# Opening a two-branch RWKV-7 and short-convolution layer on one core: the first block's inputs and projections ahead of those of the later blocks

## The chip, the cores and the metric

The kernel runs on one core of a Trainium2 chip. A core has a matrix engine (TensorE, PE in the profile), a vector engine (VectorE, DVE), a scalar engine (ScalarE, ACT), a general engine (GpSimd, POOL) and an engine that here issues all transfers (SyncE, SP). Each of them works through its own instructions in order and waits on semaphores for the others. The metric is device time in microseconds (us), lower is better; the median of the runs counts.

## What is computed

One layer of a hybrid encoder over 1152 tokens of width 1024: 1024 tokens of one prompt and 8 samples of 16 tokens. The parts that matter here:

```
h = rmsnorm(x, g_norm)
proj = h @ w_in                      # 81 column tiles of 128
pa_mix = pa + mu_shift * (pa_prev - pa)
r, k, v, w_lr, a_lr, z_a = split(pa_mix)
d = w_decay0 + tanh(w_lr) @ w_decay2         # w_lr, a_lr: 64 columns each
w = exp(-DECAY_SCALE * sigmoid(d))
a = sigmoid(w_iclr0 + a_lr @ w_iclr2)
y, S = wkv7_scan(wkv0, r, w, kh, a, v, kt)   # delta rule, 16 heads of 64
u = gc * xb ;  out_b = (gb * conv3(u) * silu(z_b)) @ w_o_b
x = x + (sigmoid(g_a) * out_a + sigmoid(g_b) * out_b) @ w_out
x = x + sigmoid(rmsnorm(x, g_ple) @ w_ple_gate) * (p @ w_ple)
```

## The kernel before

The tokens are cut into three blocks, in this order: `BLOCKS = [(0, 512), (1024, 128), (512, 512)]`, that is the first half of the prompt, all samples, the second half of the prompt. The nine input tiles `xt` (128 tokens by 1024) are normed token by token, transposed on TensorE into PSUM tiles `px`, scaled by `g_norm` and written as a high and a low half-precision part into `hx`, which stays in SBUF (`prologue`, L259 to L286). A dense product of one 128-column tile of `w_in` with one block (`dense_parts`, L162) is 8 steps over the model width with 3 matmuls each (high by high, high by low, low by high), 24 in all, 128x512 or for the samples 128x128. Their PSUM tiles are named after what they hold: `dl` the 128 columns of `w_lr` and `a_lr`, `dk`, `dr`, `dv`, `dz` those of one pair of heads, `dC`, `dx`, `dzb`, `dB` those of the convolution branch.

Every load of a weight tile (`load_w`, L143) takes one of two staging buffers `wst`, is split by ScalarE (`whi`) and VectorE (`wlo`), and frees its staging buffer after the second. `lora_in` (L288) makes from `dl` the two small factors `lrd` and `lra`, from which every later step takes its decay and its learning rate (`lod`, `loa`).

The kernel's order is: four input tiles loaded, the `dl` weights, `prologue(0)`, the weights of the first pair of heads, `cload` (constants), `lora_in(0)`, `prologue(1)`, `prologue(2)`, `lora_in(1)`, `lora_in(2)`. In this part a list scheduler places the instructions of every engine. `prologue` works there in groups of two input tiles.

Then the main stage begins (`go`, L887). For the other engines the list scheduler still decides, but TensorE's order is written by a planner: seven streams (generators) give out small pieces of work, each with the time after which its next piece may come, and the planner puts them in line by a clock `pe[0]` that it counts itself from the matmuls' sizes. Streams in order of precedence: `chain` (the serial recurrence, 144 chunks, PSUM tiles `c` and `u`), `tail` (output norm, `y` and `py`), `values`, `inverse` (`itt`, `ig`, `i`, `ie`, `if`), `scores` (`psc`), `prep` (the projections of one step, `dk`, `dr`, `dv`, `dz`), `conv` (the convolution branch, eight times). A step is one pair of heads and one block, 24 in all; a pair has 8, 2 and 8 chunks. Pieces of dense products (`DENSE`, `MORE`) fill the time in which no other piece is due. Which stream fills is a matter of pace:

```
behind = S_conv.cost / CONV_US < (chunks[0] + LEAD) / 144
fills.sort(key=lambda x: (x is S_conv) != behind)
```

`tail` waits by the planner's clock 11 us between the sum over `y` and the transposes `py`; `prep` waits before `dv` until the tail of two steps earlier is done. After the main stage come the gates (`dgb`, `dga`), the output products (`ob`, `oa`, `oc`) and the last projection (`pg`, `ple`); these are placed by the list scheduler again, and the first `dgb` products stand between the last chunks of the chain.

Of the kernel before, what the change touches and what calls it, by code (L numbers as in the profile page):

```python
# [9 lines left out]
F32 = mybir.dt.float32  # L10
# [61 lines left out]
def _build(nc, tc, I, O, top):  # L72
# [181 lines left out]
    def xload(i):  # L254
        tag, bufs = (("ar", 3), ("kbt", 2))[i % 2]
        xts[i] = wk.tile([128, D], F32, tag=tag, name=f"xt{i}", bufs=bufs)
        SP.dma_start(xts[i], I["x"][i])

    def prologue(bi):  # L259
        o, n = blk = BLOCKS[bi]  # L260
        for t0 in range(0, n // 128, 2):
            tn = min(2, n // 128 - t0)
            ms = small.tile([128, 2], F32, tag="msx", name=f"msx{bi}_{t0}")
            xs = []
            for i in range(tn):
                ti = o // 128 + t0 + i
                if ti not in xts:
                    xload(ti)
                xs.append(xts[ti])
                jk = cvp.tile([128, D], F16, tag="tb", name=f"jk{ti}", bufs=1)  # L270
                A.activation(jk, xs[i], AF.Square, accum_out=ms[:, i:i + 1])
            V.tensor_scalar(out=ms[:, :tn], in0=ms[:, :tn], scalar1=1.0 / D, scalar2=EPS, op0=ALU.mult, op1=ALU.add)
            rs = rsqrt(ms[:, :tn], tn, f"x{tn}")
            for i in range(tn):
                V.tensor_scalar(out=xs[i], in0=xs[i], scalar1=rs[:, i:i + 1], scalar2=None, op0=ALU.mult)
            sl = slice(t0 * 128, (t0 + tn) * 128)
            for k0 in range(0, KT, 2):
                ps = psp.tile([128, 2, 256], F32, tag="p", name=f"px{bi}_{t0}_{k0}")
                for k in range(2):
                    for i in range(tn):  # L280
                        PE.transpose(ps[:, k, i * 128:(i + 1) * 128], xs[i][:, (k0 + k) * 128:(k0 + k + 1) * 128], ident)
                for k in range(2):
                    hi, lo = (hT(k0 + k, blk, w)[:, sl] for w in range(2))
                    A.activation(hi, ps[:, k, :tn * 128], AF.Copy, scale=P("gn", k0 + k))
                    V.scalar_tensor_tensor(out=lo, in0=ps[:, k, :tn * 128], scalar=P("gn", k0 + k), in1=hi,
                                           op0=ALU.mult, op1=ALU.subtract)  # L286

    def lora_in(bi):  # L288
        o, n = blk = BLOCKS[bi]
        ps = dense(wl, blk, f"l{bi}")  # L290
        lm = tt(st_, "ta", f"lm{bi}", TA)[:, :n]
        mixed(ps, T_L, blk, lm, P("mu", T_L), mum[:, T_L:T_L + 1], mus[:, T_L:T_L + 1], f"l{bi}")
        A.activation(lm[0:64], lm[0:64], AF.Tanh)
        A.activation(lrd[0:64, o:o + n], lm[0:64], AF.Copy)
        A.activation(lra[64:128, o:o + n], lm[64:128], AF.Copy)
        V.tensor_tensor(out=lrd[64:128, o:o + n], in0=lm[0:64], in1=lrd[0:64, o:o + n], op=ALU.subtract)
        V.tensor_tensor(out=lra[0:64, o:o + n], in0=lm[64:128], in1=lra[64:128, o:o + n], op=ALU.subtract)

    sbd = [wk.tile([128, 128], F32, tag=f"sbd{i}", name=f"sbd{i}", bufs=1) for i in range(3)]
# [46 lines left out]
    def prep(f):  # L346
# [8 lines left out]
        smp, nch, npr, nm = f.smp, f.nch, f.npr, f.nm  # L355
        th = []
        for q, hb in (("d", 0), ("a", 1)):
            yield 2.0 * hb
            ps = psa.tile([128, 512], F32, tag="a", name="lo" + q + nm)
            lr = (lrd, lra)[hb]  # L360
            mm(ps[:, :n], s.lwh[:, hb, :], lr[:, o:o + n], start=True, stop=False)
            mm(ps[:, :n], s.lwl[:, hb, :], lr[:, o:o + n], start=False, stop=True)
            t = tt(st_, "ta", "th" + q + nm, TA)[:, :n]
            A.activation(t, ps[:, :n], AF.Tanh, scale=0.5 * IWS, bias=half[:, hb, j:j + 1])
            th.append(t)
        thd, tha = th
        G.tensor_scalar(out=thd, in0=thd, scalar1=1.0, scalar2=None, op0=ALU.add)
        cum = tt(st_, "ta", "cum" + nm, TA)[:, :n]
        sl, ns = (16, 8) if smp else (64, nch)
        V.tensor_tensor_scan(out=cum, data0=(scan_s if smp else scan_p), data1=thd, initial=0.0,  # L370
                             op0=ALU.mult, op1=ALU.add)
        pb = tt(st_, "ta", "pb" + nm, TA)[:, :ns * (sl + 1)].rearrange("p (c t) -> p c t", t=sl + 1)
        G.memset(pb[:, :, 0:1], 1.0)
        seg = lambda x: x.rearrange("p (c t) -> p c t", t=sl)
        A.activation(pb[:, :, 1:], seg(cum), AF.Exp, scale=-0.5 * CDEC)
        pt = small.tile([128, 8], F32, tag="pt", name="pt" + nm, bufs=4)
        G.tensor_copy(pt.unsqueeze(2)[:, :ns, :], pb[:, :, sl:sl + 1])
        pi = tt(st_, "ta", "pi" + nm, TA)[:, :n]
        A.activation(pi, cum, AF.Exp, scale=0.5 * CDEC)

        m = {}
        ahead = g == 2 and j + 1 < 8
        for q, t in (("k", T_K), ("r", T_R), ("v", T_V), ("z", T_ZA)):
# [14 lines left out]
            mixed(ps, t + j, blk, x, *mu, q + nm)  # L398
            m[q] = x
            if q == "r":  # L400
                x = m["k"]
# [342 lines left out]
    def conv(j):  # L744
        nm = f"{j}"
        cs = cvp.tile([128, NTOK], F32, tag="cv", name="cs" + nm, bufs=2)
        w = conv_w(j, 0)
        for o, n in BLOCKS:
            ps = yield from dense_parts(w, (o, n), f"C{nm}_{o}")
            A.activation(cs[:, o:o + n], ps, AF.Copy, scale=IWS * IWS)  # L750
        s3 = lambda x: x.rearrange("p (s t) -> p s t", t=16)
        cv = cvp.tile([128, NTOK], F32, tag="cv", name="cv" + nm, bufs=2)
        w = conv_w(j, 1)
        for o, n in BLOCKS:
            ps = yield from dense_parts(w, (o, n), f"x{nm}_{o}")
            u = cvp.tile([128, 514], F32, tag="cu", name=f"u{nm}_{o}", bufs=1)
# [20 lines left out]
        w = conv_w(j, 2)  # L777
        for o, n in BLOCKS:
            ps = yield from dense_parts(w, (o, n), f"zb{nm}_{o}")
# [5 lines left out]
        for o, n in BLOCKS:  # L785
            ps = yield from dense_parts(w, (o, n), f"B{nm}_{o}")
            V.scalar_tensor_tensor(out=zs[:, o:o + n], in0=ps, scalar=0.5 * IWS * IWS, in1=zs[:, o:o + n],
                                   op0=ALU.mult, op1=ALU.mult)
# [5 lines left out]
    for j in range(8):  # L794
        for g in range(3):
            f = St()
            f.j, f.g, f.blk, f.i, f.y_done = j, g, BLOCKS[g], len(steps), False
            f.kb_done = f.m_done = f.x_done = False
# [12 lines left out]
    prologue(1)  # L811
    prologue(2)
    lora_in(1)
    lora_in(2)

    class Stream:
        def __init__(self, kind):  # L820
            self.kind, self.at, self.gen, self.next, self.ready, self.cost = kind, 0, None, None, 0.0, 0.0
            self.till, self.banks = None, 0
            self.total = 8 if kind is conv else len(steps)

# [23 lines left out]
        def fill(self):  # L848
            return self.next in (DENSE, MORE)

    S_chain, S_tail, S_val, S_inv, S_scores, S_prep, S_conv = every = [
        Stream(k) for k in (chain, tail, values, inverse, scores, prep, conv)]
    may = {S_chain: lambda i: S_inv.at > i and S_val.at > i and S_tail.at >= i - 1,
# [3 lines left out]
           S_scores: lambda i: S_prep.at > i and (i < 3 or steps[i - 3].y_done),  # L857
           S_prep: lambda i: S_chain.at >= i - 3,
           S_conv: lambda i: True}
    CONV_US, LEAD = 8 * 46.4, 4.0  # L860

    def go():
        while True:
            for x in every:
                if x.gen is None and x.at < x.total and may[x](x.at):
                    x.gen = x.kind(x.at if x is S_conv else steps[x.at])
                    x.step()
# [318 lines left out]
```

## Time and profile before

| | |
|---|---|
| median of 3 runs | 1945.68 us (1945.39 to 3071.51) |
| profiled execution, its own time | 1941.51 us |
| its span | 1939.7 us |
| TensorE busy | 1814.9 us (94%) |
| VectorE busy | 1255.6 us (65%) |
| ScalarE busy | 811.8 us (42%) |
| mean granted TensorE clock | 0.988 |

One execution is profiled. The page gives each engine's busy time and cuts the span into 40 slices; the views of the trace give single instructions with start and length, the idle time ahead of one and what ended it (in square brackets), and the busy time of each engine in chosen stretches. "Granted clock" is the share of TensorE's full clock, 1.00 or 0.50 at a moment and a mean in between over a stretch.

### The profile page before, as it was taken

The numbers are of one execution on the slowest core, as the hardware profiler recorded it, in microseconds if no ns is written. First come the engines' busy times: TensorE is split into PE (matmuls) and PEld (weight loads), VectorE is DVE, ScalarE is ACT, GpSimd is POOL, SyncE is SP. The second block draws the span as 40 slices with busy tenths as digits, with TensorE's granted clock in tenths as the row PEclk, the third lists the DMA queues.
The fourth block names the chain that finished last, engine by engine and source line by source line (L and its number), as shares of the span: only waits on it lengthen the run. The fifth ranks groups of instructions, "written<-read, shape, count | busy, mean of one in ns | idle before, by whom it ended". The sixth has DMA issues, their size and how long they took to land. (4 is left out here: it accounts for less than half of the span.)

```text
span 1939.7 us, 37843 instructions
## 1 busy us (share of the span) xinstructions
PE 1814.9 (94%) x15374; PEld 1248.6 (64%) x15374; DVE 1255.6 (65%) x3225; ACT 811.8 (42%) x1877; POOL 219.1 (11%) x333
## 2 busy tenths in 40 slices
PE   4999999999999999999999998799999999999997
PEld 2565665565566566566556566455698777899766
DVE  7466878787787787787877777774223311444665
ACT  6344545545446446446446445343202211332321
POOL 1010211111111111111111111110000111200000
PEclk9999999999999999999999999899999999999999
DMA  6002011101101101101101100013313311142012
GB/s 217 22 23 76 22 48 42 34 30 60 39 30 50 50 30 50 50 30 37 60 29 37 41 18 15 32 46 94 99 44 96 99 44 33 56 144 87 9 35 78
DMA packets 43758, 103.57 MB, mean 53 GB/s; under 512 B 6208, under 2 KB 21440, under 8 KB 43584
## 3 DMA queue, kind: packets, MB, share of 16 engines
q1 hardware_dynamic: 43584, 101.17, 16.3%
q8 instruction: 120, 1.97, 0.4%
q14 instruction: 54, 0.44, 0.1%
HBM read 84.40 MB, written 16.74 MB: 52 GB/s over the span
## 5 line engine op out<-in xcount | busy, mean ns | idle before, releaser
L92 PEld LDWEIGHTS <-whip 128*128 128x128 f16 x1536 | 132.3, 99 | 72.2 <-issue 3.5
L653 POOL TENSOR_SCALAR Spt<-sbd,pt 128x128 f32<-128x128 f32 x128 | 86.7, 677 | 664.8 <-DVE sbd L669 642.5
L92 PEld LDWEIGHTS <-wlop 128*128 128x128 f16 x768 | 75.4, 98 | 61.1 <-issue 1.1
L669 DVE SCALAR_TENSOR_TENSOR sbd<-u,pt,Spt 64x64 f32<-64x64 f32 x256 | 72.1, 282 | 65.3 <-PE u L92 61.6
L595 ACT ACTIVATE bdgt<-ig 64x512 f16<-64x512 f32 (+1 forms) x208 | 106.5, 512 | 2.5
L659 ACT ACTIVATE yst<-c 64x128 f32<-64x128 f32 x144 | 38.8, 270 | 151.0 <-DVE xs L658 149.7
L92 PE MATMUL dx<-hx,whiX 128*128 128x512 f16 (+1 forms) x384 | 88.4, 326 | 4.7 <-ACT sho L229 4.7
L92 PE MATMUL dgb<-hx,whigb 128*128 128x512 f16 (+1 forms) x384 | 90.5, 331 | 2.2 <-ACT whigb L148 1.6
L92 PE MATMUL dv<-hx,whip 128*128 128x512 f16 (+1 forms) x384 | 90.7, 331 | 0.0
L92 PE MATMUL dzb<-hx,whiZ 128*128 128x512 f16 (+1 forms) x384 | 88.6, 326 | 2.2 <-ACT sho L229 1.8
L92 PE MATMUL dz<-hx,whip 128*128 128x512 f16 (+1 forms) x384 | 89.5, 326 | 0.0
L92 PE MATMUL dC<-hx,whiC 128*128 128x512 f16 (+1 forms) x384 | 88.4, 327 | 1.1 <-ACT cs L750 0.6
L92 PE MATMUL dB<-hx,whiB 128*128 128x512 f16 (+1 forms) x384 | 89.1, 326 | 0.0
L92 PE MATMUL pg<-xn,pg 128*128 128x384 f16 (+1 forms) x576 | 88.9, 309 | 0.0
L92 PE MATMUL dr<-hx,whip 128*128 128x512 f16 (+1 forms) x384 | 88.9, 326 | 0.0
L92 PE MATMUL dk<-hx,whip 128*128 128x512 f16 (+1 forms) x384 | 88.1, 326 | 0.0
L92 PE MATMUL dga<-hx,whiga 128*128 128x512 f16 (+1 forms) x384 | 86.9, 326 | 0.0
L92 PEld LDWEIGHTS <-pg 128*128 128x128 f16 x768 | 66.3, 99 | 27.1 <-issue 2.4
L664 ACT ACTIVATE vu<-u 64x64 f32<-64x64 f32 x288 | 62.3, 216 | 46.8 <-PE u L92 44.1
L589 ACT ACTIVATE gt<-ig 128x512 f16<-128x512 f32 (+1 forms) x104 | 54.3, 522 | 66.0 <-PE ig L92 65.1
L596 DVE CAST_PREDICATED tt<-cph,i 128x512 f16<-128x512 uint16 (+1 forms) x104 | 61.7, 593 | 25.4 <-PE i L92 24.3
L92 PEld LDWEIGHTS u<-xs,tm 128*128 128x128 f32 x288 | 49.7, 192 | 43.9 <-DVE xs L658 28.8
(325 smaller groups left out, 4924.8 us busy)
## 6 DMA issues: line engine op xcount, KB each, us to landing
wstp<-i_w_in SPq DMA_DIRECT2D x32, 512.0 KB, 3.6
xt<-i_x SPq DMA_DIRECT2D x9, 512.0 KB, 5.5
ob_d<-zb SPq DMA_DIRECT2D x8, 576.0 KB, 2.8
ostb<-ob_d SPq DMA_DIRECT2D x24, 192.0 KB, 3.1
osta<-oa_d SPq DMA_DIRECT2D x24, 192.0 KB, 2.9
xr<-i_xT SPq DMA_DIRECT2D x8, 576.0 KB, 3.6
wstC<-i_w_in SPq DMA_DIRECT2D x8, 512.0 KB, 3.5
wstX<-i_w_in SPq DMA_DIRECT2D x8, 512.0 KB, 3.5
```

The costliest lines, as they stand in the source:

```text
L92: PE.matmul(out, lhsT, rhs, start=start, stop=stop)
L589: A.activation(Gt, pg, AF.Copy, scale=-1.0)
L595: A.activation(Gb[R, :, R], pg[R], AF.Copy, scale=-1.0)
L596: V.copy_predicated(out=Tt, mask=bc(lvt[:, b, :]).bitcast(U16), data=p1)
L653: G.tensor_scalar(out=Spt, in0=S, scalar1=pt[:, c:c + 1], scalar2=None, op0=ALU.mult)
L659: A.activation(yst[Vh, p, :], pc[Vh, 0:128], AF.Copy)
L664: A.activation(vu[Uh, c, H], pu[H, H], AF.Copy, scale=-1.0)
L669: V.scalar_tensor_tensor(out=S2[H, H], in0=pu[H, 128 + h * 64:192 + h * 64], scalar=pt[H, c:c + 1], in1=Spt[H, H], op0=ALU.mult, op1=ALU.add)
```

## The change

The input tiles go to four buffer tags in place of two. `prologue` norms a whole block as one group (one sum, one reciprocal root for four tiles), scales every second tile on ScalarE, and is a generator that gives out one transposed column tile at a time. Block 0's prologue runs ahead under high priority; the `k` weights are loaded ahead of the `l` weights, then the constants, the small second factors, `C0`, `r`, the five other input tiles, `v` and `z`. An eighth stream `opening` does the rest: for block 0 it waits until `dk` of step 0 is out and does `lora_in(0)`; for the two other blocks it does their prologue and then `lora_in`. `prep` of step 0 takes `k` first and its decay part (`lod`, `loa`) after; `prep` of steps 1 and 2, the conv products of blocks 1 and 2 and `keys` wait until `opening` has come so far.

```diff
     def xload(i):
-        tag, bufs = (("ar", 3), ("kbt", 2))[i % 2]
+        tag, bufs = (("ar", 3), ("kbt", 2), ("vu", 2), ("scy", 3))[i % 4]
...
     def prologue(bi):
-        for t0 in range(0, n // 128, 2):
-            tn = min(2, n // 128 - t0)
...
+        tn = n // 128
+        ms = small.tile([128, 4], F32, tag="msx", name=f"msx{bi}")[:, :tn]
+        xs = [xts[o // 128 + i] for i in range(tn)]
...
+        rs = rsqrt(ms, tn, f"x{bi}")
+        for i in range(tn):
+            if i % 2:
+                A.activation(xs[i], xs[i], AF.Copy, scale=rs[:, i:i + 1])
+            else:
+                V.tensor_scalar(out=xs[i], in0=xs[i], scalar1=rs[:, i:i + 1], scalar2=None, op0=ALU.mult)
+        for k in range(KT):
+            yield 1.0 if k else (0.0, 9.0, 1.0)[bi], 1
+            ps = psp.tile([128, 512], F32, tag="p", name=f"px{bi}_{k}")[:, :n]
             for i in range(tn):
+                tr(ps[:, i * 128:(i + 1) * 128], xs[i][:, k * 128:(k + 1) * 128], ident)
+            hold(1.5)
+            A.activation(hT(k, blk, 0), ps, AF.Copy, scale=P("gn", k))
+            V.scalar_tensor_tensor(out=hT(k, blk, 1), in0=ps, scalar=P("gn", k), in1=hT(k, blk, 0),
+                                   op0=ALU.mult, op1=ALU.subtract)
...
     def lora_in(bi):
-        ps = dense(wl, blk, f"l{bi}")
+        yield 1.5
+        ps = yield from dense_parts(wl, blk, f"l{bi}")
...
+    def opening(i):
+        if i == 0:
+            yield lambda: steps[0].k_done
+        else:
+            yield waits[i]
+            yield from inputs[i]
+        yield from lora_in(i)
+        if i == 0:
+            inputs.extend([None, prologue(1), prologue(2)])
+            waits.extend([None, next(inputs[1]), next(inputs[2])])
...
+        def decay():
+            yield lambda: f.i or S_open.at > 0
...
+            if q == "k" and not f.i:
+                f.k_done = True
+                tha, pb, pt, pi = yield from decay()
...
-        yield lambda: f.i < 1 or steps[f.i - 1].kb_done
+        yield lambda: S_open.at == 3 and (f.i < 1 or steps[f.i - 1].kb_done)
...
         for o, n in BLOCKS:
+            yield lambda: o == 0 or S_open.at >= 2 + (o == 512)
             ps = yield from dense_parts(w, (o, n), f"C{nm}_{o}")
...
     for i in range(4):
         xload(i)
+    with tc.high_priority():
+        for _ in prologue(0):
+            pass
+    load_q(0, "k")
     wl = load_w(I["w_in"][T_L], "l")
-    prologue(0)
+    cload()
     load_lora(0)
-    for q in "krvz":
+    cws[0] = load_w(I["w_in"][T_C], "C0")
+    load_q(0, "r")
+    for i in (8, 4, 5, 6, 7):
+        xload(i)
+    for q in "vz":
         load_q(0, q)
-    cload()
-    lora_in(0)
-    prologue(1)
-    prologue(2)
-    lora_in(1)
-    lora_in(2)
...
-           S_prep: lambda i: S_chain.at >= i - 3,
+           S_prep: lambda i: S_chain.at >= i - 3 and S_open.at >= (0, 2, 3)[min(i, 2)],
+           S_open: lambda i: True,
```

The new stream stands in the planner's list between `scores` and `prep`.

What it moves on the engines is shown at three places. The first is VectorE at the very start, the reciprocal root (`nrx`, `nax`) and the scaling of the first input tiles. Before, for the group of two tiles:

```order
L138 SCALAR_TENSOR_TENSOR nax_159<-nax_159,nrx_158 128x2
L139 SCALAR_TENSOR_TENSOR nrx_158<-nax_159,nrx_158 128x2
L275 TENSOR_SCALAR xt_138<-xt_138,nrx_158 128x1024
L275 TENSOR_SCALAR xt_140<-xt_140,nrx_158 128x1024
L272 TENSOR_SCALAR msx_2_208<-msx_2_208 128x2
```

After, for the group of four:

```order
L137 TENSOR_TENSOR nax_157<-nrx_156,msx_146 128x4
L149 SCALAR_TENSOR_TENSOR wlop_8_231<-wstp_8_228,whip_8_230 128x1024
L138 SCALAR_TENSOR_TENSOR nax_157<-nax_157,nrx_156 128x4
L139 SCALAR_TENSOR_TENSOR nrx_156<-nax_157,nrx_156 128x4
L274 TENSOR_SCALAR xt_138<-xt_138,nrx_156 128x1024
L274 TENSOR_SCALAR xt_142<-xt_142,nrx_156 128x1024
L149 SCALAR_TENSOR_TENSOR wlol<-wstl,whil 128x1024
```

The split of the `k` weights now stands inside the reciprocal root, and only tiles 0 and 2 are scaled here; ScalarE scales 1 and 3 (after `whip_8` and `whil` in its own order).

The second place is TensorE where the first decay product `lod` of step 0 stands. Before, in the middle of the samples' `dl`:

```order
L92 LDWEIGHTS whil
L92 MATMUL dl_502<-hx,whil 128x128
L92 LDWEIGHTS lwh_269
L92 MATMUL lod_0_589<-lrd,lwh_269 128x512
L92 LDWEIGHTS lwl_270
L92 MATMUL lod_0_589<-lrd,lwl_270 128x512
L281 MATMUL px_0_6_375<-ident,xt_336 128x128 x2
L92 LDWEIGHTS whil
L92 MATMUL dl_502<-hx,whil 128x128
```

After, right behind the last matmul of block 0's `dl`, with `loa` and then `dr` behind it:

```order
L92 MATMUL dl_353<-hx,wlol 128x512
L92 LDWEIGHTS lwh_249
L92 MATMUL lod_0_430<-lrd,lwh_249 128x512
L92 LDWEIGHTS lwl_250
L92 MATMUL lod_0_430<-lrd,lwl_250 128x512
L92 LDWEIGHTS lwh_249
L92 MATMUL loa_0_435<-lra,lwh_249 128x512
L92 LDWEIGHTS lwl_250
L92 MATMUL loa_0_435<-lra,lwl_250 128x512
L92 LDWEIGHTS whip_0_261
L92 MATMUL dr_0_450<-hx,whip_0_261 128x512
```

So `lod` lost what stood between its input's product and itself. The third place is TensorE near the end of the main stage, where the output transposes `py` of the last pair's step before stand (`u` belongs to the chain, `ig` and `i` to the inverse). Before:

```order
L92 MATMUL u_0_1_16416<-vu_0_15726,kbt_0_15669 128x128
L92 LDWEIGHTS bdmh
L92 MATMUL ig_1_16435<-tt_1_16270,bdmh 128x64
L92 LDWEIGHTS bdmh
L92 MATMUL ig_1_16435<-tt_1_16270,bdmh 128x64
L96 MATMUL py_2_16440<-ident,yc_2_16327 128x128 x4
L92 LDWEIGHTS whip_16_14594
L92 MATMUL dv_2_16448<-hx,whip_16_14594 128x512
```

After:

```order
L92 LDWEIGHTS whiB_15629
L92 MATMUL dB_1024_16311<-hx,whiB_15629 128x128
L92 LDWEIGHTS whiB_15629
L92 MATMUL dB_1024_16311<-hx,whiB_15629 128x128
L92 LDWEIGHTS wloB_15630
L92 MATMUL dB_1024_16311<-hx,wloB_15630 128x128
L92 MATMUL u_0_1_16295<-vu_0_15492,kbt_0_15435 128x128
L96 MATMUL py_2_16321<-ident,yc_2_16155 128x128 x4
```

The last convolution product `dB` of the eighth convolution, which before was through some ten chunks earlier, now lies around this place: all 24 matmuls of its block 0, the first 6 of the samples' 24 ahead of `py`, the rest and block 2's 24 behind it.

## Rows read from the trace of the kernel before

**Rows 1.** Busy time by stretch: the stretch (us from the span's start), its length, then busy us and instructions of TensorE, its weight loads, VectorE, ScalarE and GpSimd, the granted TensorE clock, the transfer engines' share and GB/s.

```profile
0.00:26.00 26.00, 6.26 (x24) 4.57 (x25) 16.58 (x51) 14.96 (x25) 4.86 (x15) 1.00 0.79 270
26.00:60.00 34.00, 26.25 (x125) 15.64 (x125) 26.17 (x80) 22.43 (x54) 0.00 (x0) 0.85 0.30 103
60.00:160.00 100.00, 96.98 (x833) 54.78 (x832) 58.87 (x132) 42.29 (x88) 11.04 (x19) 1.00 0.11 35
160.00:1220.00 1060.00, 1003.66 (x9879) 635.52 (x9878) 836.15 (x2242) 534.24 (x1300) 158.88 (x258) 1.00 0.12 39
1220.00:1240.00 20.00, 11.78 (x100) 8.36 (x100) 15.75 (x60) 7.01 (x26) 1.71 (x2) 0.74 0.03 10
1240.00:1252.00 12.00, 11.26 (x69) 6.51 (x65) 6.71 (x18) 2.27 (x9) 1.21 (x2) 1.00 0.03 10
```

**Rows 2.** TensorE in order of time at the start: start us, length us, engine, line, operation, operands, count, and in brackets the idle time before and what ended it. The first transposes, the first dense product, the first matmul behind the last `dl`.

```profile
11.00 2.21 PE L281 MATMUL px<-ident,xt 128*128 128x128 f32 x8 [11.00 <-DVE xt L275]
...
26.05 0.59 PE L92 MATMUL dl<-hx,whil 128*128 128x512 f16 x1 [1.92 <-ACT hx L284]
...
59.97 0.38 PE L92 MATMUL dC<-hx,wloC 128*128 128x512 f16 x1
```

**Rows 3.** Groups of TensorE instructions from 0 to 60 us, shapes apart: busy us, mean ns of one, then idle us before them and what ended it. Of the three matmuls of each dense step two are `whil`, one `wlol`.

```profile
L281 PE MATMUL px<-ident,xt 128*128 128x128 f32 x72 | 16.8, 378 | 20.6 <-DVE xt L275 15.9 <-DVE hx L285 4.6
L92 PE MATMUL dl<-hx,whil 128*128 128x512 f16 x32 | 12.5, 448 | 3.2 <-ACT hx L284 2.5 <-DVE hx L285 0.7
...
L92 PE MATMUL dl<-hx,whil 128*128 128x128 f16 x16 | 3.3, 266 | 3.1 <-ACT hx L284 2.6 <-DVE hx L285 0.6
```

**Rows 4.** TensorE in order of time, to be read for the time from one start to the next: one 128x512 matmul in the first dense product, three of them a little later (two high, one low), three of 128x128, and four transposes.

```profile
27.72 0.63 PE L92 MATMUL dl<-hx,wlol 128*128 128x512 f16 x1
28.15 0.63 PE L92 MATMUL dl<-hx,whil 128*128 128x512 f16 x1
...
60.19 0.59 PE L92 MATMUL dC<-hx,whiC 128*128 128x512 f16 x2
...
60.83 0.59 PE L92 MATMUL dC<-hx,whiC 128*128 128x512 f16 x2
...
1197.48 0.28 PE L92 MATMUL dz<-hx,whip 128*128 128x128 f16 x2
...
1197.65 0.28 PE L92 MATMUL dz<-hx,whip 128*128 128x128 f16 x2
...
1245.70 0.64 PE L96 MATMUL prn<-ident,rnb 128*128 128x128 f32 x4
1246.18 0.59 PE L92 MATMUL dz<-hx,whip 128*128 128x512 f16 x2
```

**Rows 5.** The other engines at the start: ScalarE reading the sum of the fourth square, its first weight split, and a later split that waited for its load; VectorE's first step of the first reciprocal root (eleven steps), the two scalings behind it, and a weight split; SyncE's issue of the load that the later split waited for.

```profile
10.41 0.19 ACT L271 ACTIVATION_READ_ACCUMULATOR jk<-xt 128x1 f32 x1
11.04 1.06 ACT L148 ACTIVATE whil<-wstl 128x1024 f16<-128x1024 f32 x1 [0.44 <-DMA wstl<-i_w_in]
...
21.58 1.06 ACT L148 ACTIVATE whip<-wstp 128x1024 f16<-128x1024 f32 x1 [2.28 <-DMA wstp<-i_w_in]
...
8.02 0.17 DVE L272 TENSOR_SCALAR msx<-msx 128x2 f32<-128x2 f32 x1 [2.79 <-ACT jk L271]
...
10.19 1.42 DVE L275 TENSOR_SCALAR xt<-xt,nrx 128x1024 f32<-128x1024 f32 x2
...
12.20 1.23 DVE L149 SCALAR_TENSOR_TENSOR wlol<-wstl,whil 128x1024 f16<-128x1024 f32 x1
...
16.98 0.33 SPq L145 DMA_DIRECT2D wstp<-i_w_in  x1
```

**Rows 6.** From `dl` to `lod` of block 0, on ScalarE, VectorE and TensorE, each in order of time.

```profile
36.24 0.69 ACT L222 ACTIVATE lm<-dl,mum 128x512 f32<-128x512 f32 x1
...
38.17 0.62 ACT L293 ACTIVATE lm<-lm 64x512 f32<-64x512 f32 x1
...
39.47 0.63 ACT L294 ACTIVATE lrd<-lm 64x512 f16<-64x512 f32 x1
...
36.97 0.75 DVE L227 SCALAR_TENSOR_TENSOR lm<-dl,mus,lm 128x511 f32<-128x511 f32 x1
...
40.44 0.69 DVE L296 TENSOR_TENSOR lrd<-lm,lrd 64x512 f16<-64x512 f32 x1
...
41.18 0.38 PE L92 MATMUL lod<-lrd,lwh 128*128 128x512 f16 x1 [0.56 <-DVE lrd L296]
```

**Rows 7.** Busy time by stretch while transposes of block 2 stand between dense matmuls, and the stretch behind it (columns as in the first group).

```profile
48.00:56.00 8.00, 6.62 (x26) 4.11 (x26) 4.88 (x13) 4.46 (x12) 0.00 (x0) 0.57 0.00 0
56.00:60.00 4.00, 4.00 (x23) 2.03 (x22) 1.74 (x4) 1.36 (x4) 0.00 (x0) 1.00 0.00 0
```

**Rows 8.** TensorE and VectorE in order of time around `py` of the last pair: `c` products of the chain, and the transposes with their wait for the normed output `yc`.

```profile
1222.63 0.39 PE L92 MATMUL c<-sbd,ar 128*128 128x128 f32 x2
...
1236.08 1.11 PE L96 MATMUL py<-ident,yc 128*128 128x128 f32 x4 [4.84 <-DVE yc L723]
...
1239.55 0.47 PE L92 MATMUL c<-sbd,ar 128*128 128x128 f32 x2
...
1251.80 0.38 PE L92 MATMUL c<-sbd,ar 128*128 128x128 f32 x2
...
1235.35 0.68 DVE L723 TENSOR_TENSOR yc<-yc,nry 128x512 f32<-128x512 f32 x1
```

More of the change, by code (lines that the diff above doesn't have):

```diff
@@ L260, in prologue @@
         o, n = blk = BLOCKS[bi]
-        for t0 in range(0, n // 128, 2):
-            tn = min(2, n // 128 - t0)
-            ms = small.tile([128, 2], F32, tag="msx", name=f"msx{bi}_{t0}")
-            xs = []
-            for i in range(tn):
[L266 to L286, printed above, removed]
@@ new lines, in prologue @@
+        tn = n // 128
+        ms = small.tile([128, 4], F32, tag="msx", name=f"msx{bi}")[:, :tn]
+        xs = [xts[o // 128 + i] for i in range(tn)]
+        for i in range(tn):
+            jk = cvp.tile([128, D], F16, tag="tb", name=f"jk{bi}_{i}", bufs=1)
+            A.activation(jk, xs[i], AF.Square, accum_out=ms[:, i:i + 1])
+        V.tensor_scalar(out=ms, in0=ms, scalar1=1.0 / D, scalar2=EPS, op0=ALU.mult, op1=ALU.add)
+        rs = rsqrt(ms, tn, f"x{bi}")
+        for i in range(tn):
+            if i % 2:
+                A.activation(xs[i], xs[i], AF.Copy, scale=rs[:, i:i + 1])
+            else:
+                V.tensor_scalar(out=xs[i], in0=xs[i], scalar1=rs[:, i:i + 1], scalar2=None, op0=ALU.mult)
@@ L297, in lora_in @@
         V.tensor_tensor(out=lra[0:64, o:o + n], in0=lm[64:128], in1=lra[64:128, o:o + n], op=ALU.subtract)
+    def opening(i):
[8 more added lines that the diff above has]
+            waits.extend([None, next(inputs[1]), next(inputs[2])])
+    inputs, waits = [], []
     sbd = [wk.tile([128, 128], F32, tag=f"sbd{i}", name=f"sbd{i}", bufs=1) for i in range(3)]
@@ L355, in prep @@
         smp, nch, npr, nm = f.smp, f.nch, f.npr, f.nm
[L356 to L365, printed above, removed]
@@ L366, in prep @@
-        thd, tha = th
-        G.tensor_scalar(out=thd, in0=thd, scalar1=1.0, scalar2=None, op0=ALU.add)
-        cum = tt(st_, "ta", "cum" + nm, TA)[:, :n]
-        sl, ns = (16, 8) if smp else (64, nch)
[L370 to L379, printed above, removed]
+        sl, ns = (16, 8) if smp else (64, nch)
+        def decay():
+            th = []
+            yield lambda: f.i or S_open.at > 0
+            for q, hb in (("d", 0), ("a", 1)):
+                yield 2.0 * hb
+                ps = psa.tile([128, 512], F32, tag="a", name="lo" + q + nm)
+                lr = (lrd, lra)[hb]
+                mm(ps[:, :n], s.lwh[:, hb, :], lr[:, o:o + n], start=True, stop=False)
+                mm(ps[:, :n], s.lwl[:, hb, :], lr[:, o:o + n], start=False, stop=True)
+                t = tt(st_, "ta", "th" + q + nm, TA)[:, :n]
+                A.activation(t, ps[:, :n], AF.Tanh, scale=0.5 * IWS, bias=half[:, hb, j:j + 1])
+                th.append(t)
+            thd, tha = th
+            G.tensor_scalar(out=thd, in0=thd, scalar1=1.0, scalar2=None, op0=ALU.add)
+            cum = tt(st_, "ta", "cum" + nm, TA)[:, :n]
+            V.tensor_tensor_scan(out=cum, data0=(scan_s if smp else scan_p), data1=thd, initial=0.0,
+                                 op0=ALU.mult, op1=ALU.add)
+            pb = tt(st_, "ta", "pb" + nm, TA)[:, :ns * (sl + 1)].rearrange("p (c t) -> p c t", t=sl + 1)
+            G.memset(pb[:, :, 0:1], 1.0)
+            seg = lambda x: x.rearrange("p (c t) -> p c t", t=sl)
+            A.activation(pb[:, :, 1:], seg(cum), AF.Exp, scale=-0.5 * CDEC)
+            pt = small.tile([128, 8], F32, tag="pt", name="pt" + nm, bufs=4)
+            G.tensor_copy(pt.unsqueeze(2)[:, :ns, :], pb[:, :, sl:sl + 1])
+            pi = tt(st_, "ta", "pi" + nm, TA)[:, :n]
+            A.activation(pi, cum, AF.Exp, scale=0.5 * CDEC)
+            return tha, pb, pt, pi
@@ L381, in prep @@
+        if f.i:
+            tha, pb, pt, pi = yield from decay()
         m = {}
@@ L399, in prep @@
             m[q] = x
+            if q == "k" and not f.i:
+                f.k_done = True
+                tha, pb, pt, pi = yield from decay()
             if q == "r":
@@ L754, in conv @@
         for o, n in BLOCKS:
+            yield lambda: o == 0 or S_open.at >= 2 + (o == 512)
             ps = yield from dense_parts(w, (o, n), f"x{nm}_{o}")
@@ L822, in __init__ @@
             self.till, self.banks = None, 0
-            self.total = 8 if kind is conv else len(steps)
+            self.total = {conv: 8, opening: 3}.get(kind, len(steps))
         def step(self):
@@ L849, in fill @@
             return self.next in (DENSE, MORE)
-    S_chain, S_tail, S_val, S_inv, S_scores, S_prep, S_conv = every = [
-        Stream(k) for k in (chain, tail, values, inverse, scores, prep, conv)]
+    S_chain, S_tail, S_val, S_inv, S_scores, S_open, S_prep, S_conv = every = [
+        Stream(k) for k in (chain, tail, values, inverse, scores, opening, prep, conv)]
     may = {S_chain: lambda i: S_inv.at > i and S_val.at > i and S_tail.at >= i - 1,
@@ L865, in go @@
                 if x.gen is None and x.at < x.total and may[x](x.at):
-                    x.gen = x.kind(x.at if x is S_conv else steps[x.at])
+                    x.gen = x.kind(x.at if x in (S_conv, S_open) else steps[x.at])
                     x.step()
```

4 lines of the change are left out of this document (3 added, 1 removed).

## The prediction

> **What bounds the kernel now.** I read first the busy time by stretch. From 60 to 1220 us TensorE is the bound: it is busy 1003.66 of the 1060 us from 160 on, at the full clock, so 5.3% idle [rows 1], spread over small waits. The reader should see two places that stand out. In the first 60 us TensorE works for 32.5 us and much of that slowly; from 1220 to 1240 it is busy 11.78 of 20 us, at a mean clock of 0.74 [rows 1]. Then I read TensorE in order of time at both places, and the other engines beside it, to see who is late. What lies between is a long stretch in which the time is the matmul work plus a few per cent.
>
> So the sum is kept in one currency, the time lost: time passed, less the work that TensorE has done at its full clock. Work that only changes its place costs nothing; what is lost less is gained.
>
> Prices at the full clock come from the time between starts [rows 4]. Three 128x512 matmuls take 0.64 us (60.19 to 60.83), so 0.216 each; at the half clock one takes 0.43 (27.72 to 28.15). Three of 128x128 take 0.17 us, 0.057 each; four transposes 0.48, 0.12 each.
>
> **Lost at the start, before.** The first transposes start at 11.00, the first dense matmul at 26.05, and at 59.97 the last `dl` is through [rows 2]. By then TensorE has done all 72 transposes and the `dl` of the three blocks, 48 large and 24 small matmuls [rows 3], and by its order two `lod` and two `dC`: 72 x 0.12 + 52 x 0.216 + 24 x 0.057 = 21.2 us of work. Lost: 59.97 - 21.2 = 38.8 us. The transposes alone waited 20.6 us for scaled inputs and PSUM [rows 3].
>
> **Lost at the start, after.** The loads of the four tiles are the same, so the fourth square's sum is there at 10.6 [rows 5]. The first reciprocal root took from 8.02 to 10.19 for its eleven steps [rows 5]; now it starts at 10.7, and a weight split of 1.23 us stands in it, which waits for ScalarE's 1.06 us on the same weights (11.04 to 12.1, as `whil` before) and fits in at about 12.5. The root ends at 14.1; VectorE scales two tiles in 1.42, ScalarE (1.06 for a like tile [rows 5]) two from 14.1 to 16.2. First transposes at 14.8, so 3.8 later than before, and the first column tile is complete at about 16.6.
>
> From there eight column tiles go through two PSUM banks; each costs ScalarE about 0.69 and VectorE 0.75 (its nearest 128x512 rows [rows 6]). VectorE has between them two weight splits (1.23 each), one small one and the tail of the samples' sum: 6.0 + 2.5 + 0.6, from 17.3 to about 27. The `dC` weights: their load now waits for the `k` split to free a staging buffer (13.8); a load in this stretch took 16.98 to 21.58, 4.6 us [rows 5], so they are there at 18.4 and split by 22.3. `dC` can start at 21.5, waits a moment for the low weights, is paced by the last column tiles and starts at the half clock like the first `dl` (0.43): I take its end at 31. Work by then: 32 x 0.12 + 24 x 0.216 = 9.0; lost 22.0. That is 16.8 us less.
>
> Some of it is given back, because `opening` has little to fill with:
> - `lod` stands right behind `dl`. From ScalarE's start on `dl` to `lod` it took 36.24 to 41.18, 4.9 us, with a little foreign work in it [rows 6]. Before, TensorE filled this and waited 0.56; now nothing stands between. Queued behind `lod` are `loa`, `dr` and all else of TensorE, and the later engines wait with it. Price 4.7.
> - After a stop of 4.84 us at 1231 the matmuls from 1236.08 to 1239.55 ran at half speed [rows 8]. I expect the same in `dr`: half of 3.5, 1.8 us.
> - Behind `dr` stand three transposes, then the sums `pss`, which need ScalarE's mixed `r` (0.69, it stands ahead on ScalarE) and a square of like length, with two small evictions: about 2.2 against 0.4 us of transposes. Price 1.8.
> - The samples' `dl` waits for their last column tile behind `v`: 0.5. Block 2's transposes stand between `dz` matmuls; VectorE has there 8 evictions and some ten operations of `keys`, 13 us against TensorE's 9, but `dl` of block 2 fills behind: 1.5.
>
> Lost by the end of the third `dl`: 22.0 + 10.3 = 32.3 against 38.8, so the start gives **6.5 us**. Both ends: nothing, if the `dC` weights come some 6 us later, and 16.8 - 4.7 = 12 if the wait for `lod` is all that is given back.
>
> **The middle.** By the order, TensorE has between the first chunks of the third, fourth, fifth and sixth pair the same dense matmuls before and after (401, 392, 392, 392 large ones, 196 small). The chain only comes earlier: ahead of its first chunk stand 320 large dense matmuls in place of 386. Since TensorE and not the chain is the bound here, I cost this at nothing; what hides it is the dense work itself, and should the chain become the bound, rival 2's price is due. The fewer small operations (three reciprocal roots in place of five, 24 evictions an engine in place of 40) lie on engines that are 50 and 79% busy there [rows 1]: nothing.
>
> **The hole at 1220.** Before, the convolution branch is through by then, `dv` of the last step may not start before the tail two steps earlier is done, and TensorE stands for the chain and then 4.84 us for `yc`, which VectorE finishes at 1236.03 [rows 8]. From 1220 to 1252 TensorE is busy 23.0 of 32, so 9.0 idle [rows 1]. A mean clock of 0.74 over 20 us is 10.4 us at half, about 5 of them busy, so 2.5 us of work lost: 11.5 in all. Of this 1.7 (5.3% of 32) is usual and stays: at most 9.8 to gain. After, 48 large and 24 small `dB` matmuls, 11.7 us, are left for just this place, 24 and 6 of them ahead of `py`. They took their time earlier before, so what they fill here is saved there. The least: `py` still waits its 4.84 and 1.7 follow at the half clock, so 3.3. I take **8**, near the upper end, because VectorE's long list ahead of `yc` came from the next step's keys, whose `pss` now stands behind the chain's second chunk. The chain can follow: over the last pair's first six chunks TensorE now has 107 large dense matmuls by its order, 23 us, in place of 62, and a chunk there took 6.1 us with matmuls between (1239.55 to 1251.80 is two [rows 8]), 37 for six.
>
> What comes next is as before: `dz` of the last step ends at the chain's fifth chunk of that step in both orders, and the gates' weights follow it.
>
> **The sum.** 6.5 + 8 = 14.5 us. The profiled execution has a span of 1939.7 and a time of 1941.51: 1927.0. The median of the runs is 4.2 above that execution, so for the median **1931**.
>
> **Rivals.**
> 1. The start gives nothing: the change delays the first transposes, the `C0` load stands behind a staging buffer, and the first dense matmul comes so late that the waits eat it all. For it: constants and five input tiles are queued around it, and the transfer engines are 79% busy up to 26 us [rows 1]. Against it: a load took only 4.6 us there. It leaves the 8 us of the hole: 1938.
> 2. The hole stays, because `yc` is late for another reason: 6.5 + 3.3, 1936.
> 3. Slower: the clock does not come back after `lod`. From 48 to 56, with transposes of block 2 woven between matmuls, the mean clock was 0.57 though TensorE was busy 83%; it came back only once the matmuls stood unbroken, 1.00 from 56 on [rows 7]. After `lod` come pieces like these: `dr`, `dv`, `dz`, the samples' products, 28 transposes and the third `dl`, some 27 us of work. All at half: 27 - 1.8 = 25 more, 25 - 14.5 = 11 slower than before, 1956. It decides from 16 us of work at the half clock on. Against it: `dr` is 24 matmuls without a break, and 3.5 us sufficed at 1236. The Trainium skill has a rule for this, "TensorE: Matmul & The Clock Gate", section "A second HAM failure mode: psum-queue depth-cycling": a matmul stream that cycles through PSUM banks with short idle times between its groups lets the clock fall and rise again and again. By that rule the time is this rival's. The trace agrees in that loose stretch (0.57) and not in the main stage, where 5.3% of small idle times leave the clock at 1.00.
> 4. More: both terms at their upper ends, 12 + 9.8: 1924.
>
> **How the numbers follow.** Forecast 0.57 (its own range 1925 to 1938), rival 1 0.18, rival 2 0.10, rival 3 0.10, rival 4 0.05. Rival 3 and the tails are left out: 1920 to 1946. 2% (39 us), about what a measurement of this kernel can tell from no change, lies outside every case, since the change touches 100 of 1940 us; a disturbance that I do not see is left 0.03 for faster and 0.02 for slower, and 0.95 for within 2%.
>
> **What would show it.** In the profile after: first transposes near 15 and `dC` from 21 to 31; a wait of `lod` for `lrd` of 4 to 5 us near 42, with 0.43 us matmuls behind it for 3 to 4 us (longer: rival 3); the chain's first chunk some 20 us earlier, two thirds of it only by order; `py` of the last pair waiting under 2 us and `dB` rows around it (else rival 2); the first `dgb` about 15 us earlier. The prediction is wrong if the middle from first chunk to last pair takes more than before for the same matmuls, or if `dC` starts after 28.

## The result and the profile after

The kernel after takes 1931.52 us (median of 4 runs, 1930.34 to 1933.24), beside 1945.54 for the kernel before on the same chip. One of the four runs of before took 3071.51 us in a disturbed state and stays out of the ratio; the other three lie between 1942.16 and 1945.68. The ratio is 0.993, with a 95% interval of 0.9913 to 0.9948. On another chip (the last run of the next section) it was 0.9948, interval 0.9931 to 0.9965. So the change is faster by about 10 to 14 us, and within 2%. The execution that was profiled took 1932.12 us with a span of 1930.3, which is 9.4 us less than the span of before; the places below are looked for in these 9.4 us, so they are read from one execution of each kernel. The forecast was 1931 with a range of 1920 to 1946, so the time came where it was put. Its terms did not all come where they were put.

The start, by TensorE in order of time, answers to [rows 2, 3, 6].

```profile
14.55 2.12 PE L96 MATMUL px<-ident,xt 128*128 128x128 f32 x8 [14.55 <-DVE xt L274]
...
22.47 1.06 PE L92 MATMUL dC<-hx,whiC 128*128 128x512 f16 x2
...
29.08 0.59 PE L92 MATMUL dk<-hx,whip 128*128 128x512 f16 x2
...
43.97 0.53 PE L92 MATMUL lod<-lrd,lwh 128*128 128x512 f16 x1 [4.37 <-DVE lrd L294]
...
45.56 1.06 PE L92 MATMUL dr<-hx,whip 128*128 128x512 f16 x2
...
53.73 0.33 PE L96 MATMUL px<-ident,xt 128*128 128x128 f32 x1 [1.66 <-DVE hx L282]
...
55.39 1.06 PE L92 MATMUL dv<-hx,whip 128*128 128x512 f16 x2
...
83.20 0.22 PE L92 MATMUL lod<-lrd,lwh 128*128 128x128 f16 x1
```

The first transposes start at 14.55, `dC` is through when `dk` begins at 29.08, `lod` waits 4.37 us, and `dr` behind it runs at the half clock (1.06 for two). A second stretch at the half clock stands in `dv`, from 55.39. The third `dl` ends ahead of the row at 83.20, with 50.0 us of work done, so 33.2 us are lost, beside 38.8 before.

The end of the serial chain, by stretch (columns as in [rows 1]), answers to the last two rows there; the same stretches of before follow where [rows 1] does not have them.

```profile
1180.00:1200.00 20.00, 19.47 (x212) 13.00 (x208) 15.07 (x37) 11.75 (x28) 6.11 (x8) 1.00 0.01 2
1200.00:1220.00 20.00, 19.96 (x174) 12.53 (x173) 15.05 (x59) 8.30 (x30) 2.53 (x4) 1.00 0.01 3
1220.00:1240.00 20.00, 20.00 (x147) 12.11 (x148) 13.66 (x35) 4.72 (x16) 1.82 (x3) 1.00 0.11 43
1240.00:1260.00 20.00, 14.83 (x160) 9.20 (x154) 13.23 (x32) 9.22 (x21) 1.81 (x3) 0.83 0.35 113
```

The kernel before:

```profile
1180.00:1200.00 20.00, 18.26 (x233) 13.59 (x230) 16.22 (x55) 12.70 (x32) 2.20 (x3) 1.00 0.08 32
1200.00:1220.00 20.00, 16.95 (x164) 10.34 (x165) 14.32 (x35) 11.29 (x29) 5.55 (x8) 1.00 0.00 1
```

From 1200 to 1240 TensorE is now busy 39.96 of 40 us and always at the full clock; `py` starts without a wait. Before, it was idle not only in the hole that the prediction looked at but already for 1.7 and 3.0 us of the two stretches ahead of it.

What follows, TensorE after, in order of time: `py`, the first `dgb`, and a single `ob` matmul a hundred microseconds later; last, SyncE's issue of the load of its weights `w_ob`. This `py` and that of [rows 8], called `py` of the last pair there, are the transposes of the seventh pair's third block, the 21st step of 24; they stand beside the first chunks of the last pair.

```profile
1219.63 0.60 PE L96 MATMUL py<-ident,yc 128*128 128x128 f32 x4
...
1244.07 0.49 PE L92 MATMUL u<-xs,tm 128*128 128x128 f32 x2 [2.95 <-DVE xs L680]
...
1247.92 1.25 PE L92 MATMUL dgb<-hx,whigb 128*128 128x512 f16 x4 [1.60 <-ACT whigb L148]
...
1352.43 0.66 PE L92 MATMUL ob<-ohb,wohb 128*128 128x384 f32 x1 [3.91 <-issue]
1352.88 1.08 PE L92 MATMUL dgb<-hx,whigb 128*128 128x512 f16 x2
...
1347.76 0.33 SPq L937 DMA_DIRECT2D wstb<-i_w_ob  x1
```

The kernel before at the same places:

```profile
1260.17 1.25 PE L92 MATMUL dgb<-hx,whigb 128*128 128x512 f16 x4 [1.60 <-ACT whigb L148]
...
1363.45 0.41 PE L92 MATMUL ob<-ohb,wohb 128*128 128x384 f32 x1 [1.21 <-issue]
...
1358.84 0.33 SPq L908 DMA_DIRECT2D wstb<-i_w_ob  x1
```

The first `dgb` comes 12.25 us earlier, yet the span is shorter by only 9.4. The largest loss behind it is at `ob`: this one matmul stands alone between `dgb` products in TensorE's order and waits 3.91 us (1.21 before; `issue` means that the profile names nothing that it waited for), and the `dgb` behind it runs at the half clock.

**Where the time went.** The ledger below keeps the prediction's currency, the time lost: time at a mark, less the matmul work that TensorE's order has ahead of it, at the prices of [rows 4] and, for the small products, at times between starts read in the same way. Under each mark stand its times before and after. "First py" and "20th py" are the transposes of step 0 and of the samples of the seventh pair; 20 steps of 24 are through by then.

| lost at | before | after | gained so far | in this part |
|---|---|---|---|---|
| end of third `dl` (59.97; 83.2) | 38.8 | 33.2 | 5.6 | +5.6 |
| first `py` (231.1; 210.6) | 49.1 | 46.7 | 2.4 | -3.2 |
| 20th `py` (1170.6; 1149.8) | 149.8 | 152.5 | -2.7 | -5.1 |
| first `dgb` (1260.17; 1247.92) | 179.4 | 166.7 | 12.7 | +15.4 |
| end of the span | | | 9.4 | -3.3 |

So what the opening gained was gone by the 20th `py`, and in this ledger the end of the chain gave the whole of the gain.

### The profile page after: what moved, and what is told of

Read it like the earlier page. It is cut to its first block, busy times and chain, and to the rows that moved or that the text cites. A ratio compares the mean times of both kernels' runs of the same rounds, so it can differ in the third digit from the quotient of the medians.

```text
span 1930.3 us, 37773 instructions
## 1 busy us (share of the span) xinstructions
PE 1811.0 (94%) x15374; PEld 1246.8 (65%) x15374; DVE 1246.8 (65%) x3183; ACT 815.0 (42%) x1865; POOL 212.7 (11%) x333
## 4 chain that ended last, share of the span: by engine, by line
PE 69%; DVE 17%; ACT 7%; issue 3%; DMA 2%; POOL 0%; POOLq 0%; SPq 0%; DVEq 0%; ACTq 0%
PE ob L92 5%; PE oc L92 5%; PE dga L92 5%; PE dr L92 4%; PE dz L92 4%; PE oa L92 4%; PE dk L92 4%; PE dv L92 4%; PE dB L92 4%; PE pg L92 4%; PE dC L92 4%; PE u L92 3%; PE dzb L92 3%; PE dgb L92 3%; PE dx L92 2%
## 5 line engine op out<-in xcount | busy, mean ns | idle before, releaser
L92 PE MATMUL u<-xs,tm 128*128 128x128 f32 x288 | 60.7, 292 | 21.9 <-DVE xs L680 21.0
```

Of the source, the lines that this page charges most:

```text
L92: PE.matmul(out, lhsT, rhs, start=start, stop=stop)
```

## Experiments

Theory A: the gain comes from work left for the end of the chain, and that is left because the chain starts earlier in TensorE's order. Rival: the gain is the earlier start itself, and what happens at the end adds little. Ratios are against the kernel before, run on the same chip; the first four runs shared one chip, the last four another.

**1. The pace alone, in the kernel before**

```
-    CONV_US, LEAD = 8 * 46.4, 4.0
+    CONV_US, LEAD = 8 * 46.4, -8.0
```

> The kernel before with its opening, and only LEAD lowered from 4 to -8, so that by the order 48 large dense matmuls more (10 us of work) stand from chunk 114 on, 39 of them in chunks 120 to 125; the kernel after leaves 96 more. Theory (the larger part of the gain is work left for the end of the chain): about half of the hole is filled without any new opening, 4 to 7 us faster than before, about 1939 to 1941. Rival (the gain comes from the earlier start): no change, 1945.

Measured: 1953.18 us, ratio 1.0058 (1.0045 to 1.0072). Neither theory has this: it is 11 us slower. By stretch, the hole did fill (TensorE busy 18.06 of 20 us, before 11.78):

```profile
1220.00:1240.00 20.00, 18.06 (x169) 10.80 (x167) 14.10 (x40) 7.28 (x25) 1.42 (x3) 1.00 0.09 32
```

But 168.7 us were already lost at the 20th `py` (before 149.8). From the list of waits between 85 and 1200 us (us in total, times, longest):

```profile
PE py L96 <- DVE yc L723: 14.1, 7, 4.3
```

The same line of before:

```profile
PE py L96 <- DVE yc L723: 4.1, 5, 1.7
```

The pace that fills the hole is paid for in the middle, among others with 10 us more of waits of `py`. `LEAD` does not act at the end alone: the chain's first chunk, too, came at 154.3 us here (160.9 before). A fuller end is not worth much unless the middle stays as it was. Where the rest of the 19 us went was not followed up.

**2. The opening of after, with the old end**

```
-    CONV_US, LEAD = 8 * 46.4, 4.0
+    CONV_US, LEAD = 8 * 46.4, 12.0
```

> The kernel after with its opening, and only LEAD raised from 4 to 12: the convolution branch is through at chunk 122 by the order, as before the change, and no dB matmul is left for the hole. Theory (the larger part is work left for the end): the hole comes back and its 13 us are lost, of which the about 6 that the middle had lost return: 1938 to 1941. Rival (the gain is the opening's): the time stays within 2 us of the kernel after, 1930 to 1933.

Measured: 1943.09 us, ratio 1.0015 (1.0004 to 1.0026), so 1.7 us slower than before, the opening notwithstanding. From 1220 to 1240 the hole is back, and `py` waits as it did before the change:

```profile
1220.00:1240.00 20.00, 10.81 (x100) 7.98 (x101) 16.81 (x66) 7.82 (x29) 2.38 (x4) 0.77 0.01 3
```

```profile
1237.88 1.11 PE L96 MATMUL py<-ident,yc 128*128 128x128 f32 x4 [4.84 <-DVE yc L745]
```

The rival falls. The chain's early start alone is not it either: its first chunk came at 135.2 us here, earlier than the 140.2 of after, with the same 312 large dense matmuls ahead of it. The time is even 2 us above theory A's range; 151.4 us were lost at the 20th `py`, so raising `LEAD` gave back only 1.1 us of the middle's loss.

**3. The wait of `lod` filled**

```
             if q == "k" and not f.i:
                 f.k_done = True
+                yield lambda: S_open.at > 0
+            if q == "r" and not f.i:
                 tha, pb, pt, pi = yield from decay()
```

> The kernel after, but dr of the first step stands between dl and lod/loa in TensorE's order, so that the wait of 4.4 us of lod for lrd is filled and the half clock behind it (1.7 us) does not come. Theory: both are gained, 1924 to 1927. Rival (the stretch behind it waits for the same decay factors and the chain takes it back): 1930 to 1932.

Measured: 1928.78 us, ratio 0.9941 (0.9928 to 0.9955). That lies between the two ratios of after (0.993 and 0.9948), so the times by themselves do not show a gain over after. In the profile the first `dgb` comes at 1245.22, 2.7 us ahead of after. TensorE in order of time:

```profile
45.05 0.38 PE L92 MATMUL lod<-lrd,lwh 128*128 128x512 f16 x1
...
49.67 0.33 PE L96 MATMUL px<-ident,xt 128*128 128x128 f32 x1 [3.37 <-DVE hx L282]
...
51.48 1.86 PE L92 MATMUL pss<-cpk,sq 128*128 128x2 f32 x8 [1.48 <-ACT sq L429]
...
53.45 1.06 PE L92 MATMUL dv<-hx,whip 128*128 128x512 f16 x2
```

The wait of 4.37 is gone and `dr` is at the full clock. Half of it comes back a few instructions on: the transposes' wait grows from 1.66 to 3.37 and `pss` now waits 1.48. My reading, not tried, is that ScalarE and VectorE have the same list to work off and TensorE only comes to it sooner. The stretch at the half clock in `dv` stays. By the profile the gain lies between the two expectations.

**4. "As one group" undone**

```
+        gs = 4 if bi else 2
+        for t0 in range(0, tn, gs):
```

(and below it the squares, the root and the scaling of each group of `gs` tiles)

> The kernel after, but the first block's four tiles are normed as two groups of two, as before the change; the wide projections still come at once. Theory (the first dC is bound by its weights, there at 21 to 22): the first transposes come some 3 us earlier and dC does not, within 1 us of the kernel after. Rival (one group sets the start of dC): 3 us slower or faster.

Measured: 1932.56 us, ratio 0.9958 (0.9945 to 0.997). The first transposes start at 10.99 in place of 14.55, and `dC` at 21.72 in place of 22.47. So `dC` moved as little as expected, but not for the reason given: the weights of `C0` were split by ScalarE at 20.81, and `dC` followed 0.9 us later, right behind a group of transposes that stand ahead of it in TensorE's order. Grouping is worth no more than a microsecond at this place. The median cannot be set against after's to a microsecond, since they ran on different chips.

**5. dB moved into the hole, in the kernel before**

```
         w = conv_w(j, 3)
         for o, n in BLOCKS:
+            yield lambda: j < 7 or chunks[0] >= 126
```

> The kernel before, with its opening and its order up to the last pair; only the last convolution's dB products (48 large, 24 small) are held until chunk 126, so that they stand around py of the last pair. They leave chunks 120 to 126 thinner, since nothing else is there to fill. Theory A (what closes the hole is work that is left because the chain started earlier in TensorE's order, 312 large dense matmuls ahead of it in place of 378; without that the hole only moves some chunks ahead): at most 3 us faster than before, 1938 to 1945. Rival B (dB in that place is enough, no opening needed): 8 to 13 us faster, 1929 to 1935.

Measured: 1946.81 us, ratio 1.0016 (1.0004 to 1.0028); the profiled execution is the fastest of its runs, 1941.78. Rival B falls: the products stand at `py`, which does not wait, and the time is not better. It is 2 us above theory A's range too. The hole has moved ahead, by stretch:

```profile
1200.00:1220.00 20.00, 14.85 (x139) 10.33 (x137) 14.84 (x49) 8.99 (x25) 2.62 (x5) 0.79 0.00 1
1220.00:1240.00 20.00, 19.82 (x156) 12.60 (x157) 13.66 (x43) 5.85 (x23) 1.20 (x2) 0.87 0.01 2
```

173.4 us were lost at the 21st `py`, that of [rows 8], beside 170.3 before.

**6. The opening of after, with the chain started where it was**

```
-    may = {S_chain: lambda i: S_inv.at > i and S_val.at > i and S_tail.at >= i - 1,
+    may = {S_chain: lambda i: (i or S_conv.cost >= 36) and S_inv.at > i and S_val.at > i and S_tail.at >= i - 1,
```

> The kernel after with its opening and LEAD 4; only the chain's first chunk is held until the convolution branch has had 36 us, so that 375 large dense matmuls stand ahead of it (before: 378, after: 312). By the order dB is then through at chunk 122, as before the change. Theory A: the hole comes back and the gain is gone, 1939 to 1945. Rival (the gain is the earlier dense work of the opening): within 3 us of the kernel after, 1929 to 1935.

Measured: 1941.94 us, ratio 0.999 (0.9977 to 1.0004): no difference from before. This is as theory A has it. The opening is whole and `LEAD` is untouched; only the chain's first chunk waits until 375 large dense matmuls stand ahead of it. At the end of the third `dl` the run is 4.8 us ahead of before in the ledger, at the first `py` only 0.9 (48.2 lost, before 49.1), and at the 20th `py` 6.1 (143.7 lost, before 149.8). So the opening's gain did not simply last: most of it was gone by the first `py`, and the stretch to the 20th gained 5.2 anew, about 1.5 of it a fall of the clock that before had and this run has not (last section). Then the hole takes 4.0 of the 6.1. TensorE by stretch and in order of time:

```profile
1220.00:1240.00 20.00, 12.77 (x63) 8.16 (x64) 12.19 (x45) 5.47 (x20) 1.71 (x2) 0.54 0.04 14
```

```profile
1233.24 1.11 PE L96 MATMUL py<-ident,yc 128*128 128x128 f32 x4 [4.85 <-DVE yc L745]
...
1258.04 1.25 PE L92 MATMUL dgb<-hx,whigb 128*128 128x512 f16 x4 [2.22 <-ACT whigb L148]
```

`py` waits 4.85 us again (4.84 in [rows 8]), and the first `dgb` is 2.1 us ahead of before, 10.1 behind after.

**7. The best version**

Run 3's edit, and the weights of the first `w_ob` column tile asked for three column tiles earlier:

```
     for j in range(KT):
         gate(ms[j], T_GB + j, f"b{j}")
+        if j == 4:
+            w_ob0 = load_wr(I["w_ob"][0], "b0")
         obs.append(load_o(ob_d, j, f"b{j}"))
     for j in range(KT):
-        w = load_wr(I["w_ob"][j], f"b{j}")
+        w = load_wr(I["w_ob"][j], f"b{j}") if j else w_ob0
```

> The kernel after, with dr of the first step between dl and lod as in the third run, and the load and split of the first w_ob weights asked for three column tiles earlier, so that no single ob matmul waits among the dgb products. Theory: 2.7 us from the first (measured there at the first dgb) and 3.9 of wait with some 3 of half clock from the second: 9 us faster than the kernel after, 1921 to 1925. Rival (the loads behind w_ob come later by as much and the next stage waits): 1927 to 1930.

Measured: 1924.9 us, ratio 0.99 (0.9881 to 0.9919), 8.2 us faster than the kernel after beside it (run 8). By the order no `ob` matmul stands among the `dgb` products any more. The load is issued at 1295.92 (after: 1347.76), and the stretch that answers to the wait, with after's beside it, reads

```profile
1341.00:1356.00 15.00, 14.74 (x92) 7.54 (x91) 8.63 (x13) 9.03 (x17) 0.00 (x0) 1.00 0.69 223
```

```profile
1345.00:1360.00 15.00, 10.82 (x55) 5.07 (x53) 8.21 (x13) 8.35 (x15) 0.00 (x0) 0.77 0.59 188
```

From run 3's profile to this one the first `dgb` gains 1.25 us and the span 8.0, so 6.75 lie behind the first `dgb`. By the ledger, read on, 5.7 of them are gained by the last `dgb`; that is the price of the `ob` wait with its half clock. The other microsecond lies far behind it, where run 3 had one fall of the clock more.

**8. The kernel after once more**

> The kernel after once more, on the chip of these runs, as the measure for the runs beside it: 1930 to 1934.

Measured: 1933.09 us, ratio 0.9948 (0.9931 to 0.9965).

## Why the prediction was right in the time and not in its terms

**The start: right, in mechanism and size.** 6.5 was forecast, 5.6 measured. `dC` ran from 22.47 to 29.08 with 20.1 us lost (forecast: 21.5 to 31, 22.0). The wait of `lod` was 4.37 (4.7) and `dr`'s half clock cost 1.7 (1.8). That price came from a row read too simply: before, the clock was at 0.50 from 1230 to 1231 already, ahead of the stop that ends at 1236.08 [rows 8]. What the list of give-backs did not have is the second half-clock stretch, in `dv`, about 2.9 us. Rival 1, that the start gives nothing, is wrong up to here. What the start gave did not reach the end, however: the middle took more than that.

**The middle, "I cost this at nothing": the step that failed.** It cost 8.3 us, 3.2 to the first `py` and 5.1 to the 20th. The reason given, the same dense matmuls between the chunks, was true and did not suffice: the order in which they stand between the chain's pieces is another, and they leave other waits. Run 6 shows that in the second part the early chain makes the loss, and not the opening: with the same opening and a late chain the middle lost 95.5 us between the two marks, after 105.8, before 100.7. The list of waits between 85 and 1200 us (us in total, times, longest) says which waits grew, after and then before:

```profile
PE u L92 <- DVE xs L680: 18.1, 16, 2.1
PE c L92 <- DVE sbd L691: 11.6, 10, 2.7
```

```profile
PE u L92 <- DVE xs L658: 13.1, 20, 1.8
PE c L92 <- DVE sbd L669: 7.5, 9, 1.2
```

These are the chain's own products; in run 6 they stand at 13.1 and 7.6 again. The two grew by 9.1 us, so other waits gave some of it back. Some 3 of the 5.1 are the clock, which such waits can lower; the last section counts them. The first part is not the early chain's: run 6 loses 3.9 there, and what makes it was not tried. The prediction had named a middle that takes more for the same matmuls as a sign that it is wrong, and by this ledger that sign came.

**The hole: right in mechanism, mis-sized.** The term was 8, with 9.8 as its most; measured are 15.4 from the 20th `py` to the first `dgb`. "From 1220 to 1252" was the error. Work left for the end fills more than the stretch in which its lack is plainest: before, 1180 to 1220 already had 4.8 us idle, after it has 0.6, and from 1256.8 to beyond the first `dgb` the clock was at half again. A loss has to be counted over all the time in which the work that is missing would have been there. Runs 2 and 6 take the filling away in two ways and both times lose the gain; run 5 shows that placing `dB` there is not the cause by itself. What has to be there is more work left altogether. In the kernel after the chain's earlier place in the order leaves it; run 2 shows that the pace can spend it again.

**"What comes next is as before": wrong by 3.3 us.** TensorE came to its `ob` matmul 13.7 us earlier (1348.5 in place of 1362.2, the starts less the waits), and the load of `w_ob` was issued only 11.1 earlier, since SyncE issues it behind the loads of `ob_d`. In both kernels `ob` starts 4.6 to 4.7 us after that issue. In run 7, where the load is asked for earlier, the lone `ob` matmul and its wait are gone.

So the sum was 14.5 us, and the profile gave 5.6 - 3.2 - 5.1 + 15.4 - 3.3 = 9.4. For the profiled execution the forecast was 1927.0 and the time 1932.12, 5.1 too low; that it was not further off is luck, since two errors of some 7 and 8 us, at the hole and in the middle, cancelled. The hit on the median is luck too: the forecast added the 4.2 us by which the median of before stood above its profile, the median of after stood 0.6 below its own, and these 4.8 us cover nearly all of the 5.1. On the chip of run 8 the median of before, 1943.0, stood only 1.5 above that profile.

**The rivals.** 2 (the hole stays) is wrong: `py` has no wait. 3 (the clock does not come back) is wrong: the clock fell twice behind `lod` and rose again each time, `dv` from 61.68 on at 0.59 for two. The rule of the Trainium skill that stood beside it, "TensorE: Matmul & The Clock Gate", section "A second HAM failure mode: psum-queue depth-cycling", expects falls and rises, and the trace agrees that far (a mean of 0.87 from 26 to 60 us); it was the price put to it, all at half, that nothing here bears out. 4 (both at their upper ends) had the right sign for the hole and not for the start.

## What to carry to other kernels

Where a serial chain and a pool of free work share an engine, look at what is left of the pool when the chain is alone: starting the chain earlier in the order can be worth more than the waits that are removed at the start, if the pace of the pool does not spend the work before the end; here the gain showed a thousand microseconds later. When work is placed anew, cost the small waits between its pieces and the clock they may lower, even where the sum of work between two marks is the same. And follow each gain to the next stage's loads, since they need not come earlier by as much as the stage does.

## What the runs showed of the hardware

**The same wait lowers the clock in one execution and not in the next.** The kernel after was profiled twice. Both times the chain's `c` waits 2.72 us at about 261 us, with the same work before and behind it. The first execution, then the second, TensorE in order of time:

```profile
263.72 0.49 PE L92 MATMUL c<-sbd,ar 128*128 128x128 f32 x2 [2.72 <-DVE sbd L691]
264.04 0.40 PE L92 MATMUL i<-gt,bdtn 128*128 128x64 f16 x8
264.27 0.60 PE L92 MATMUL dzb<-hx,whiZ 128*128 128x512 f16 x2
...
264.92 0.59 PE L92 MATMUL dzb<-hx,whiZ 128*128 128x512 f16 x2
```

```profile
263.39 0.49 PE L92 MATMUL c<-sbd,ar 128*128 128x128 f32 x2 [2.72 <-DVE sbd L691]
263.72 0.40 PE L92 MATMUL i<-gt,bdtn 128*128 128x64 f16 x8
263.95 0.81 PE L92 MATMUL dzb<-hx,whiZ 128*128 128x512 f16 x2
...
264.98 1.06 PE L92 MATMUL dzb<-hx,whiZ 128*128 128x512 f16 x2
```

The first stays at the full clock, the second falls to the half. A fall is here one such stretch at the half clock. Runs 3, 4, 7, 8 and the kernel after have the same TensorE order from the first `py` to the first `dgb`, so the time from the first to the 20th `py` can be set beside the number of such falls between them:

| | after | run 3 | run 4 | run 7 | run 8 |
|---|---|---|---|---|---|
| falls | 3 | 3 | 5 | 1 | 4 |
| us from first to 20th `py` | 939.2 | 938.9 | 942.4 | 936.6 | 941.3 |

About 1.5 us for a fall (5.8 us between one and five). Run 4 shows what that does to a small gain: it was 1.8 us ahead of after at the third `dl` (81.44) and 1.2 behind at the first `dgb`, with nothing in its order to explain it. Before had one such fall in this stretch, run 6 none. The waits ahead of these falls were of 1.5 to 2.7 us. So such a wait in a busy stretch is a chance of 1.5 us more, and two profiles that differ by 3 us need not differ in their kernels. What decides whether the clock falls stays open. The Trainium skill, "TensorE: Matmul & The Clock Gate", section "What's actually happening", says of the slow start of a kernel that its length varies from run to run. The two executions here differ in mid-kernel instead, by one fall more in the second, of which the sentence does not speak.
